# Row softmax on one core: one loop over a ring of twelve groups, a first load of 16 rows a partition, and late loads together behind two stores

## The chip, the core and the metric

The kernel runs on one core of a Trainium2 chip. The metric is device time in microseconds (us) of one execution of the program. The page and the trace of the profiled execution count from that execution's first instruction; their last instant is called the span.

The engines that matter: VectorE (DVE in the profile) does row maxima, reciprocals and most of the scaling; ScalarE (ACT) does the exponentials; GpSimd (POOL) does some of the scaling; SyncE (SP) issues every load and store; TensorE (PE) computes nothing and is used only for synchronization.

## The reference

The computation is a softmax along the last axis of a float32 array of 16 x 1024 rows with 512 elements each, 33.55 MB in and as much out.

```python
def reference(x):                                   # x: (16, 1024, 512) float32
    x_max = np.max(x, axis=-1, keepdims=True)
    exp_x = np.exp(x - x_max)
    return exp_x / np.sum(exp_x, axis=-1, keepdims=True)
```

## The kernel before

The 16,384 rows are cut into 16 groups. A group is 8 rows on each of the 128 partitions, 2 MB. Consecutive groups are bundled into chunks (`SIZES`), and a chunk is what one load and one store move: 2 MB or 4 MB. Everything stays in place: the load writes a group's rows into SBUF, the exponential and the scaling overwrite them, and the store reads them.

Four steps are done for each group.

- `rowmax` (line 145, VectorE): the negated maxima of 8 rows, or of 16 rows at once for the chunks that `WHOLE` names. It waits for the chunk's load.
- `exp` (line 134, ScalarE): eight activations, one for each row of a partition, with the negated maximum as bias and the row's sum as a second output. In the trace each is an ACTIVATE and an ACTIVATION_READ_ACCUMULATOR.
- the reciprocal of the sums (line 159, VectorE), which waits until ScalarE has finished the group (`summed`).
- the multiplication of the rows by the reciprocals (line 164), on GpSimd for the groups in `ON_POOL` and on VectorE for the others. It waits for the reciprocal (`inverted`).

Group 0 has a tensor of its own, `first`, and code of its own: its maxima are line 186, its eight exponentials are written out in front of the loop, and its reciprocal (line 211), its multiplication (line 213) and its store come at the very end. The other 15 groups go through `ring`, which holds 11 groups. ScalarE handles them in a loop (`exps`, line 150), in which one iteration is one group.

The order on VectorE is written out by hand: in step g it takes the maxima of group g (unless they were taken with those of the group before) and then scales group g - 2 (`BEHIND`). A multiplication that belongs to GpSimd is issued there at that same point.

All loads and stores go through SP's one queue, in an order written out by hand. The first load is moved in front of the starting barrier (`loads_at_the_head`). The next six loads fill the ring. Then comes `ORDER`: stores as their chunks become ready, and between them the two late loads (chunks 7 and 8), which go to places in the ring that an earlier store must have emptied (`BEFORE`). SP handles one thing after another, so whatever stands behind a wait of SP waits as well. A store waits for two counts, `by_vector` and `by_pool`, of the multiplications that are done.

At the end SP waits for all the stores (`others`, line 219).

Of the kernel before, what the change touches and what calls it, by code (L numbers as in the profile page):

```python
# [7 lines left out]
F32 = mybir.dt.float32  # L8
EXP = mybir.ActivationFunctionType.Exp
AX = mybir.AxisListType.X  # L10
ACT, DVE, POOL, PE, SP = [
    getattr(mybir.EngineType, e) for e in ("Activation", "DVE", "Pool", "PE", "SP")
]


GROUP = 8


SIZES = [1, 2, 2, 2, 2, 2, 1, 2, 2]
CHUNKS = len(SIZES)  # L20
RING = 11
STARTS = [sum(SIZES[:k]) for k in range(CHUNKS)]
GROUPS = sum(SIZES)

BEFORE = {7: 1, 8: 2}

ORDER = [
    ("store", 1),
    ("store", 2),
    ("load", 7),  # L30
    ("store", 3),
    ("load", 8),
    ("store", 4),
    ("store", 5),
    ("store", 6),
# [4 lines left out]
ON_POOL = [2, 4, 6, 8, 10, 12]  # L40

BEHIND = 2

WHOLE = (3, 4, 5)


AT_HEAD = {mybir.EngineType.SP: 1}
# [22 lines left out]
@with_exitstack  # L70
def kernel(
    ctx: ExitStack,
    tc: tile.TileContext,
    x: bass.AP,
    out: bass.AP,
):
    nc = tc.nc
    nc.at_finalize(loads_at_the_head)
    P = nc.NUM_PARTITIONS

    x_rows, out_rows = x.flatten_outer_dims(), out.flatten_outer_dims()
    d = x_rows.shape[1]
    assert x_rows.shape[0] == P * GROUPS * GROUP

    first = ctx.enter_context(nc.sbuf_tensor("first", [P, GROUP * d], F32))
    ring = ctx.enter_context(nc.sbuf_tensor("ring", [P, RING * GROUP * d], F32))

    def columns(name, n):
        return ctx.enter_context(nc.sbuf_tensor(name, [P, n], F32))


    first_stat, first_recip = columns("first_stat", GROUP), columns("first_recip", GROUP)
    stat, recip = columns("stat", RING * GROUP), columns("recip", RING * GROUP)

    def sem(name):
        return ctx.enter_context(nc.semaphore(name))

    maxima, summed, inverted, by_vector, by_pool = [
        sem(s) for s in ("maxima", "summed", "inverted", "by_vector", "by_pool")
    ]  # L100
    loaded = {k: sem(f"loaded{k}") for k in range(CHUNKS)}

    stored = {k: sem(f"stored{k}") for k in BEFORE.values()}
    others = sem("others")

    def at(g):
        return (g - 1) % RING

    def rows(g, groups=1):
        if g == 0:  # L110
            part = first[:, :]
        else:
            part = ring[:, at(g) * GROUP * d : (at(g) + groups) * GROUP * d]
        return part.rearrange("p (r d) -> p r d", d=d)

    def cols(t, g, groups=1):
        return t[:, at(g) * GROUP : (at(g) + groups) * GROUP]

    def in_dram(t, k):
        part = t[P * GROUP * STARTS[k] : P * GROUP * (STARTS[k] + SIZES[k]), :]  # L120
        return part.rearrange("(p r) d -> p r d", p=P)

    def load(k):
        return nc.sync.dma_start(  # L124
            out=rows(STARTS[k], SIZES[k]), in_=in_dram(x_rows, k)
        )

    def store(k):
        return nc.sync.dma_start(
            out=in_dram(out_rows, k), in_=rows(STARTS[k], SIZES[k])  # L130
        )

    def exp(row, one):
        return nc.scalar.activation(  # L134
            out=row, in_=row, func=EXP, bias=one, scale=1.0, accum_out=one
        )

    def spread(t):
        return t.unsqueeze(2).to_broadcast([P, GROUP, d])


    def rowmax(g, groups):
        k = max(c for c in range(CHUNKS) if STARTS[c] <= g)
        nc.vector.wait_ge(loaded[k], 16)
        nc.vector.reduce_max(  # L145
            out=cols(stat, g, groups), in_=rows(g, groups), axis=AX, negate=True
        ).then_inc(maxima, groups)

    def exps():
        with nc.Fori(0, GROUPS - 1, 1, engines=(ACT,)) as g:  # L150
            nc.scalar.wait_ge(maxima, 1).then_inc(maxima, -1)  # L151
            row = nc.scalar.snap((g % RING) * GROUP)
            for r in range(GROUP):
                done = exp(ring[:, bass.ds((row + r) * d, d)], stat[:, bass.ds(row + r, 1)])
            done.then_inc(summed, 1)

    def scale(g):
        nc.vector.wait_ge(summed, g)
        nc.vector.reciprocal(out=cols(recip, g), in_=cols(stat, g)).then_inc(inverted, 1)  # L159
        engine, scaled = nc.vector, by_vector  # L160
        if g in ON_POOL:
            engine, scaled = nc.gpsimd, by_pool
        engine.wait_ge(inverted, g)
        engine.tensor_mul(  # L164
            out=rows(g), in0=rows(g), in1=spread(cols(recip, g))
        ).then_inc(scaled, 1)

    def store_scaled(k):
        groups = STARTS[k] + SIZES[k] - 1
        on_pool = sum(g <= groups for g in ON_POOL)  # L170
        nc.sync.wait_ge(by_vector, groups - on_pool)
        if on_pool:
            nc.sync.wait_ge(by_pool, on_pool)  # L173
        store(k).then_inc(stored.get(k, others), 16)

    with tc.manual_schedule(engines={ACT, DVE, POOL, SP}):
        head = load(0)
        head.then_inc(loaded[0], 16)
        tc.info.no_tile_sem_insts.add(head.ins.name)
        nc.scalar.preload_act_table(EXP)  # L180
        with tc.tile_critical(sync_engine=SP):  # L181
            for k in range(1, min(BEFORE)):
                load(k).then_inc(loaded[k], 16)
        nc.vector.wait_ge(loaded[0], 16)
        behind = [
            nc.vector.reduce_max(  # L186
                out=first_stat[:], in_=rows(0), axis=AX, negate=True
            )
        ]
        for r in range(GROUP):  # L190
            behind.append(exp(rows(0)[:, r, :], first_stat[:, r : r + 1]))
        with tc.tile_critical(sync_engine=PE):  # L192
            exps()
            seen = 1
            for g in range(1, GROUPS):
                if g == seen:
                    k = max(c for c in range(CHUNKS) if STARTS[c] <= g)
                    take = SIZES[k] if k in WHOLE else 1
                    rowmax(g, take)
                    seen += take  # L200
                if g > BEHIND:
                    scale(g - BEHIND)
            for g in range(GROUPS - BEHIND, GROUPS):
                scale(g)
            for what, k in ORDER:
                if what == "store":
                    store_scaled(k)
                else:
                    nc.sync.wait_ge(stored[BEFORE[k]], 16)
                    load(k).then_inc(loaded[k], 16)  # L210
        nc.vector.reciprocal(out=first_recip[:], in_=first_stat[:])  # L211
        behind.append(
            nc.vector.tensor_mul(out=rows(0), in0=rows(0), in1=spread(first_recip[:]))  # L213
        )
        behind.append(store(0))
        for one in behind:
            tc.declare_no_dep(one.ins, head.ins, reason="VectorE waits for loaded[0]")
        with tc.tile_critical(sync_engine=SP):
            nc.sync.wait_ge(others, 16 * (CHUNKS - 1 - len(stored)))


# [28 lines left out]
```

## Time and profile before

| | |
|---|---|
| median of 3 runs | 161.96 us (161.93 to 162.73) |
| the profiled execution: time / span | 162.86 us / 161.1 us |
| VectorE busy | 122.9 us (76%), 39 instructions |
| ScalarE busy | 92.5 us (57%), 257 instructions |
| GpSimd busy | 42.3 us (26%), 10 instructions |
| the DMA queue | 67.11 MB, 97.5% of 16 engines' span, mean 417 GB/s |

A row of the slices has 40 digits; each is the busy share of one slice of the span, in tenths, and a slice is about 4 us long. A row of a timeline gives start, duration, engine, source line, operation, what is written and read with its shape, and in brackets the idle time of the engine before it and what ended it. A row of the waits gives who waited for whom, then the total in us, how often, and the longest. "SPq" is SP's queue of DMA issues. Durations of overlapping instructions of one engine can overlap by about 0.1 us.

### The profile page before, as it was taken

To read this page: it belongs to the slowest core of one execution; us is meant where nothing else is said; L and a number is where in the kernel's file an instruction comes from. 1 tells how busy PE (TensorE), PEld (TensorE's weight loads), DVE (VectorE), ACT (ScalarE), POOL (GpSimd) and SP (SyncE) were. 2 spreads that over 40 slices of the span, in tenths; PEclk is the share of its full clock that TensorE was granted. 3 is DMA by queue.
4 is the path that set the end of the run, shared out by engine and by line. 5 is a ranking of instruction groups with operands and counts; after the bars stand their busy time and mean duration, and the time that the engine had idled before them with its cause. 6 is when DMAs were issued, how large, how long until landed. Compare 5 with 4: busy or idle time off the path is not lost.

```text
span 161.1 us, 611 instructions
## 1 busy us (share of the span) xinstructions
DVE 122.9 (76%) x39; ACT 92.5 (57%) x257; POOL 42.3 (26%) x10
## 2 busy tenths in 40 slices
DVE  0190599999999999999999999963999999900000
ACT  3009439998957995995999919970199600000000
POOL 0000000000970690393096019500295000000000
DMA  7999999999999999999999999999999999999990
GB/s 232 435 505 391 407 505 391 407 496 399 407 488 407 399 378 500 407 399 496 407 399 488 415 391 472 439 391 464 439 399 456 399 435 468 448 399 448 395 439 28
DMA packets 2592, 67.11 MB, mean 417 GB/s; under 512 B 288, under 2 KB 288, under 8 KB 288
## 3 DMA queue, kind: packets, MB, share of 16 engines
q1 hardware_dynamic: 2592, 67.11, 97.5%
HBM read 33.55 MB, written 33.55 MB: 417 GB/s over the span
## 4 chain that ended last, share of the span: by engine, by line
DMA 47%; DVE 30%; issue 5%; POOL 4%; SPq 0%; DVEq 0%
DMA ring<-in_x_dram 35%; DVE stat L145 14%; DMA out_dram<-ring 13%; DVE ring L164 13%; POOL ring L164 4%; DVE first L213 3%; DVE recip L159 1%; SPq L124 0%; DVE first_recip L211 0%; DVEq L192 0%; SPq L245 0%; DVEq L211 0%; SPq L173 0%; SPq L181 0%
## 5 line engine op out<-in xcount | busy, mean ns | idle before, releaser
L134 ACT ACTIVATE ring<-ring,stat x120 | 84.8, 709 | 24.2 <-ACTq L151 24.2
L145 DVE TENSOR_REDUCE stat<-ring 128x8 f32<-128x4096 f32 (+1 forms) x12 | 65.4, 5457 | 10.2 <-ACT first L134 6.0
L164 POOL TENSOR_TENSOR ring<-ring,recip 128x4096 f32<-128x4096 f32 x6 | 42.1, 7016 | 80.4 <-DVE recip L159 80.4
L164 DVE TENSOR_TENSOR ring<-ring,recip 128x4096 f32<-128x4096 f32 x9 | 47.4, 5266 | 0.3
L134 ACT ACTIVATION_READ_ACCUMULATOR ring<-ring,stat x120 | 22.6, 188 | 0.0
L134 ACT ACTIVATE first<-first,first_stat 128x512 f32<-128x512 f32 x8 | 5.7, 708 | 10.0 <-DVE first_stat L186 10.0
L186 DVE TENSOR_REDUCE first_stat<-first 128x8 f32<-128x4096 f32 x1 | 4.4, 4420 | 7.6 <-DMA first<-in_x_dram 7.6
L213 DVE TENSOR_TENSOR first<-first,first_recip 128x4096 f32<-128x4096 f32 x1 | 4.4, 4424 | 0.0
L159 DVE RECIPROCAL recip<-stat 128x8 f32<-128x8 f32 x15 | 2.9, 192 | 0.0
L180 ACT ACT_TABLE_LOAD x1 | 1.3, 1283 | 0.8 <-PEq L234 0.8
L134 ACT ACTIVATION_READ_ACCUMULATOR first<-first,first_stat 128x1 f32 x8 | 1.5, 187 | 0.0
L211 DVE RECIPROCAL first_recip<-first_stat 128x8 f32<-128x8 f32 x1 | 0.2, 203 | 0.2 <-issue 0.2
L234 POOL MEMSET const-float32-0.0<- 128x1 f32 x1 | 0.1, 98 | 0.2 <-issue 0.2
L234 POOL MEMSET const-bfloat16-1.0<- 128x1 bf16 x1 | 0.1, 102 | 0.0
L234 POOL MEMSET const-uint8-127<- 128x1 uint8 x1 | 0.1, 102 | 0.0
L234 POOL MEMSET const-float32-1.0<- 128x1 f32 x1 | 0.1, 98 | 0.0
## 6 DMA issues: line engine op xcount, KB each, us to landing
ring<-in_x_dram SPq DMA_DIRECT2D x7, 4096.0 KB, 30.1
out_dram<-ring SPq DMA_DIRECT2D x7, 4096.0 KB, 23.7
first<-in_x_dram SPq DMA_DIRECT2D x1, 2048.0 KB, 7.6
ring<-in_x_dram SPq DMA_DIRECT2D x1, 2048.0 KB, 57.9
out_dram<-ring SPq DMA_DIRECT2D x1, 2048.0 KB, 28.1
out_dram<-first SPq DMA_DIRECT2D x1, 2048.0 KB, 18.4
```

Of the source, the lines that this page charges most:

```text
L134: return nc.scalar.activation(out=row, in_=row, func=EXP, bias=one, scale=1.0, accum_out=one)
L145: nc.vector.reduce_max(out=cols(stat, g, groups), in_=rows(g, groups), axis=AX, negate=True).then_inc(maxima, groups)
L159: nc.vector.reciprocal(out=cols(recip, g), in_=cols(stat, g)).then_inc(inverted, 1)
L164: engine.tensor_mul(out=rows(g), in0=rows(g), in1=spread(cols(recip, g))).then_inc(scaled, 1)
L180: nc.scalar.preload_act_table(EXP)
L186: nc.vector.reduce_max(out=first_stat[:], in_=rows(0), axis=AX, negate=True)
L211: nc.vector.reciprocal(out=first_recip[:], in_=first_stat[:])
L213: nc.vector.tensor_mul(out=rows(0), in0=rows(0), in1=spread(first_recip[:]))
L234: nc = _bacc.Bacc("TRN2", target_bir_lowering=False, num_devices=1)
```

## The change

Group 0 loses its separate tensor and code. The ring holds 12 groups, all 16 groups go through ScalarE's loop, and group 0 takes the same path as the others, so its store is now the first one. The chunks are cut anew: the first load brings two groups (16 rows a partition), and chunks 0 to 4 begin on even groups. Before, chunks 1 to 5 began on odd groups. The chunks whose maxima are taken at once are now 3 and 4, groups 6 and 7, and 8 and 9; before they were groups 5 and 6, 7 and 8, and 9 and 10. The groups on GpSimd and the lag of two groups stay.

In SP's order, stores 0 and 1 come first, and then the three late loads (chunks 7, 8 and 9: four groups) in a row: load 7 waits for store 0, and loads 8 and 9 for store 1. The other stores follow. A store waits for one semaphore of its own chunk, which VectorE and GpSimd both count up.

The last store is issued behind the hand-written part. PE then waits for all stores but that one, two of them covered by the late loads' waits; the last one is waited for by the framework. The seven early loads are no longer a block with a synchronization of its own.

The order of VectorE's and GpSimd's instructions in the middle of the two programs reads as follows ("max(5,6)" is one maximum over the 16 rows of both groups).

```
before:  max(5,6)  recip 3  VectorE mul 3   recip 4 -> GpSimd mul 4   max(7,8)  recip 5  VectorE mul 5   recip 6 -> GpSimd mul 6
after:   max(6,7)  recip 4 -> GpSimd mul 4  recip 5  VectorE mul 5    max(8,9)  recip 6 -> GpSimd mul 6  recip 7  VectorE mul 7
```

```diff
@@ -15,21 +15,23 @@
 
 GROUP = 8
 
-
-SIZES = [1, 2, 2, 2, 2, 2, 1, 2, 2]
+SIZES = [2, 2, 2, 2, 2, 1, 1, 2, 1, 1]
+RING = 12
 CHUNKS = len(SIZES)
-RING = 11
 STARTS = [sum(SIZES[:k]) for k in range(CHUNKS)]
 GROUPS = sum(SIZES)
 
-BEFORE = {7: 1, 8: 2}
+BEFORE = {7: 0, 8: 1, 9: 1}
+
 
 ORDER = [
+    ("store", 0),
     ("store", 1),
+    ("load", 7),
+    ("load", 8),
+    ("load", 9),
     ("store", 2),
-    ("load", 7),
     ("store", 3),
-    ("load", 8),
     ("store", 4),
     ("store", 5),
     ("store", 6),
@@ -41,7 +43,7 @@
 
 BEHIND = 2
 
-WHOLE = (3, 4, 5)
+WHOLE = (3, 4)
 
 
 AT_HEAD = {mybir.EngineType.SP: 1}
@@ -82,35 +84,32 @@
     d = x_rows.shape[1]
     assert x_rows.shape[0] == P * GROUPS * GROUP
 
-    first = ctx.enter_context(nc.sbuf_tensor("first", [P, GROUP * d], F32))
-    ring = ctx.enter_context(nc.sbuf_tensor("ring", [P, RING * GROUP * d], F32))
-
-    def columns(name, n):
+    def sbuf(name, n):
         return ctx.enter_context(nc.sbuf_tensor(name, [P, n], F32))
 
-
-    first_stat, first_recip = columns("first_stat", GROUP), columns("first_recip", GROUP)
-    stat, recip = columns("stat", RING * GROUP), columns("recip", RING * GROUP)
+    ring = sbuf("ring", RING * GROUP * d)
+
+    stat = sbuf("stat", RING * GROUP)
+    recip = sbuf("recip", RING * GROUP)
 
     def sem(name):
         return ctx.enter_context(nc.semaphore(name))
 
-    maxima, summed, inverted, by_vector, by_pool = [
-        sem(s) for s in ("maxima", "summed", "inverted", "by_vector", "by_pool")
-    ]
+    maxima, summed, inverted = [sem(s) for s in ("maxima", "summed", "inverted")]
+    scaled = {k: sem(f"scaled{k}") for k in range(CHUNKS)}
     loaded = {k: sem(f"loaded{k}") for k in range(CHUNKS)}
 
-    stored = {k: sem(f"stored{k}") for k in BEFORE.values()}
+    stored = {k: sem(f"stored{k}") for k in set(BEFORE.values())}
     others = sem("others")
 
+    def chunk_of(g):
+        return max(k for k in range(CHUNKS) if STARTS[k] <= g)
+
     def at(g):
-        return (g - 1) % RING
+        return g % RING
 
     def rows(g, groups=1):
-        if g == 0:
-            part = first[:, :]
-        else:
-            part = ring[:, at(g) * GROUP * d : (at(g) + groups) * GROUP * d]
+        part = ring[:, at(g) * GROUP * d : (at(g) + groups) * GROUP * d]
         return part.rearrange("p (r d) -> p r d", d=d)
 
     def cols(t, g, groups=1):
@@ -140,14 +139,13 @@
 
 
     def rowmax(g, groups):
-        k = max(c for c in range(CHUNKS) if STARTS[c] <= g)
-        nc.vector.wait_ge(loaded[k], 16)
+        nc.vector.wait_ge(loaded[chunk_of(g)], 16)
         nc.vector.reduce_max(
             out=cols(stat, g, groups), in_=rows(g, groups), axis=AX, negate=True
         ).then_inc(maxima, groups)
 
     def exps():
-        with nc.Fori(0, GROUPS - 1, 1, engines=(ACT,)) as g:
+        with nc.Fori(0, GROUPS, 1, engines=(ACT,)) as g:
             nc.scalar.wait_ge(maxima, 1).then_inc(maxima, -1)
             row = nc.scalar.snap((g % RING) * GROUP)
             for r in range(GROUP):
@@ -155,50 +153,36 @@
             done.then_inc(summed, 1)
 
     def scale(g):
-        nc.vector.wait_ge(summed, g)
+        nc.vector.wait_ge(summed, g + 1)
         nc.vector.reciprocal(out=cols(recip, g), in_=cols(stat, g)).then_inc(inverted, 1)
-        engine, scaled = nc.vector, by_vector
-        if g in ON_POOL:
-            engine, scaled = nc.gpsimd, by_pool
-        engine.wait_ge(inverted, g)
+        engine = nc.gpsimd if g in ON_POOL else nc.vector
+        engine.wait_ge(inverted, g + 1)
         engine.tensor_mul(
             out=rows(g), in0=rows(g), in1=spread(cols(recip, g))
-        ).then_inc(scaled, 1)
+        ).then_inc(scaled[chunk_of(g)], 1)
 
     def store_scaled(k):
-        groups = STARTS[k] + SIZES[k] - 1
-        on_pool = sum(g <= groups for g in ON_POOL)
-        nc.sync.wait_ge(by_vector, groups - on_pool)
-        if on_pool:
-            nc.sync.wait_ge(by_pool, on_pool)
+        nc.sync.wait_ge(scaled[k], SIZES[k])
         store(k).then_inc(stored.get(k, others), 16)
 
     with tc.manual_schedule(engines={ACT, DVE, POOL, SP}):
-        head = load(0)
-        head.then_inc(loaded[0], 16)
-        tc.info.no_tile_sem_insts.add(head.ins.name)
         nc.scalar.preload_act_table(EXP)
-        with tc.tile_critical(sync_engine=SP):
-            for k in range(1, min(BEFORE)):
-                load(k).then_inc(loaded[k], 16)
-        nc.vector.wait_ge(loaded[0], 16)
-        behind = [
-            nc.vector.reduce_max(
-                out=first_stat[:], in_=rows(0), axis=AX, negate=True
-            )
-        ]
-        for r in range(GROUP):
-            behind.append(exp(rows(0)[:, r, :], first_stat[:, r : r + 1]))
+
+
+        for k in range(min(BEFORE)):
+            first = load(k).then_inc(loaded[k], 16)
+            tc.info.no_tile_sem_insts.add(first.ins.name)
+            tc.add_to_no_dep_group("loads", first.ins)
+        tc.declare_fence(nc.sync.nop().ins, group="loads")
         with tc.tile_critical(sync_engine=PE):
             exps()
-            seen = 1
-            for g in range(1, GROUPS):
+            seen = 0
+            for g in range(GROUPS):
                 if g == seen:
-                    k = max(c for c in range(CHUNKS) if STARTS[c] <= g)
-                    take = SIZES[k] if k in WHOLE else 1
+                    take = SIZES[chunk_of(g)] if chunk_of(g) in WHOLE else 1
                     rowmax(g, take)
                     seen += take
-                if g > BEHIND:
+                if g >= BEHIND:
                     scale(g - BEHIND)
             for g in range(GROUPS - BEHIND, GROUPS):
                 scale(g)
@@ -208,15 +192,10 @@
                 else:
                     nc.sync.wait_ge(stored[BEFORE[k]], 16)
                     load(k).then_inc(loaded[k], 16)
-        nc.vector.reciprocal(out=first_recip[:], in_=first_stat[:])
-        behind.append(
-            nc.vector.tensor_mul(out=rows(0), in0=rows(0), in1=spread(first_recip[:]))
-        )
-        behind.append(store(0))
-        for one in behind:
-            tc.declare_no_dep(one.ins, head.ins, reason="VectorE waits for loaded[0]")
-        with tc.tile_critical(sync_engine=SP):
-            nc.sync.wait_ge(others, 16 * (CHUNKS - 1 - len(stored)))
+            nc.sync.wait_ge(scaled[CHUNKS - 1], SIZES[CHUNKS - 1])
+        store(CHUNKS - 1)
+        with tc.tile_critical(sync_engine=PE):
+            nc.tensor.wait_ge(others, 16 * (CHUNKS - 1 - len(stored)))
 
 
 # ---- launch: one core; inputs and outputs as the reference has them ----
```

## The prediction

> **What bounds the kernel now.** I read the slices of the page first, then the queue line, then what the queue's engine waited for, then the timelines of VectorE and GpSimd.
>
> ```profile
> DVE  0190599999999999999999999963999999900000
> POOL 0000000000970690393096019500295000000000
> DMA  7999999999999999999999999999999999999990
> GB/s 232 435 505 391 407 505 391 407 496 399 407 488 407 399 378 500 407 399 496 407 399 488 415 391 472 439 391 464 439 399 456 399 435 468 448 399 448 395 439 28
> q1 hardware_dynamic: 2592, 67.11, 97.5%
> ```
>
> The DMA row has no slice under 9 between the first and the last: one queue moves 33.55 MB in and 33.55 MB out without a hole. VectorE, busy 122.9 us of 161.1, is the second; it has idle slices at both ends and a dip near 105 us. So the end is set by bytes as long as every store is ready before the queue runs dry; compute matters only by the deadlines it sets for stores.
>
> ```profile
> DVE stat L145 <- DMA ring<-in_x_dram: 4.2, 2, 4.0
> SPq L245 <- DMA out_dram<-first: 17.8, 1, 17.8
> ```
>
> The first line (waits) says VectorE stood 4.0 us for a late load, so it was ahead of the queue there. The second (the queue's own waits): SP had issued the last store 17.8 us before it landed. That is the slack at the end of the kernel before.
>
> The pace: the first load (2 MB) lands at 7.59, the third at 26.96 in the chain (five 2 MB units in), so one unit takes (26.96 - 7.59)/4 = 4.84 us. The last store lands at 159.7 (issued 141.25, 18.4 to landing), 1.4 us before the span's end.
>
> ```profile
> 66.68 0.20 DVE L159 RECIPROCAL recip<-stat 128x8 f32<-128x8 f32 x1
> 66.80 8.63 DVE L145 TENSOR_REDUCE stat<-ring 128x16 f32<-128x8192 f32 x1
> 75.35 0.19 DVE L159 RECIPROCAL recip<-stat 128x8 f32<-128x8 f32 x1
> 75.57 4.42 DVE L164 TENSOR_TENSOR ring<-ring,recip 128x4096 f32<-128x4096 f32 x1
> 79.92 0.20 DVE L159 RECIPROCAL recip<-stat 128x8 f32<-128x8 f32 x1
> 80.03 4.37 DVE L145 TENSOR_REDUCE stat<-ring 128x8 f32<-128x4096 f32 x1
> 84.31 0.19 DVE L159 RECIPROCAL recip<-stat 128x8 f32<-128x8 f32 x1
> 84.54 6.95 DVE L164 TENSOR_TENSOR ring<-ring,recip 128x4096 f32<-128x4096 f32 x1
> 91.41 4.41 DVE L145 TENSOR_REDUCE stat<-ring 128x8 f32<-128x4096 f32 x1
> ```
>
> ```profile
> 66.96 7.01 POOL L164 TENSOR_TENSOR ring<-ring,recip 128x4096 f32<-128x4096 f32 x1 [6.22 <-DVE recip L159]
> 80.19 7.02 POOL L164 TENSOR_TENSOR ring<-ring,recip 128x4096 f32<-128x4096 f32 x1 [6.22 <-DVE recip L159]
> ```
>
> This is the row that decides. A GpSimd multiply starts 0.27 us after the reciprocal that frees it (66.68 to 66.96) and takes 7.02. The double maximum at 66.80 runs its usual 8.63 beside it. But VectorE's multiply at 84.54 meets the GpSimd one of 80.19 and takes 6.95 in place of 4.42: it ends at 91.49, which is 4.28 after GpSimd's end (87.21). The same holds at 100.35 (GpSimd ends 103.02, VectorE 107.30) and at 120.22 (122.89, 127.17). So VectorE's multiply does not share: it stands until GpSimd is through. In the kernel before, groups 4, 6 and 8 pay none of this, since a double maximum covers each of these GpSimd multiplies.
>
> **The change, part by part.**
>
> *First load of 16 rows.* 4 MB instead of 2: VectorE's first maximum starts at 7.59 + 4.84 = 12.43. Against that, VectorE no longer stands 6.02 us (to 18.03) until the eight separate exponentials are done. The queue starts as before.
>
> *One loop on ScalarE.* Same 128 exponentials, 5.65 us a group (22.81 to 28.46), 0.3 to 0.4 us from maximum to first exponential. ScalarE has 92.5 us of work; below, each reciprocal is checked against it and it is never last. Cost nothing.
>
> *Stores count per chunk.* One semaphore wait on SP instead of two, behind a full queue: nothing.
>
> *The order of VectorE and GpSimd.* The six groups on GpSimd stay 2 to 12 in steps of two, but chunks now begin on even groups. So a double maximum (groups 6,7, then 8,9) is followed by the reciprocals of groups 4 and 5 back to back, GpSimd's multiply of group 4, and VectorE's multiply of group 5 with nothing between: they start almost together. From the reciprocal of group 4: GpSimd + 0.27. VectorE: the next instruction issues 0.11 behind a reciprocal (66.68 to 66.80), and the multiply 0.23 behind its own reciprocal's start (75.35 to 75.57), so + 0.34. GpSimd is first by 0.07 us. I take it that the first holds the other off whole, as in the three rows above.
>
> No row shows so near a tie. Bounded: VectorE loses at most 7.02 (a whole GpSimd multiply) less the 0.07, at least 0 (it goes first and GpSimd stands). I take the loss, by the rows in which the one that started earlier won. The Trainium skill ("SBUF — State Buffer", section "Who interferes with whom") says that of a VectorE operation with two SBUF inputs and a GpSimd one that reads SBUF, the one issued first keeps the shared port for its whole instruction. By that rule 0.07 us is enough, and it gives the same sum; only the other order of issue would give that of the first rival below, and no row here shows who wins a tie.
>
> VectorE's clock, then, with 4.33 from a single maximum to the next instruction (80.03 to 84.31 and alike), 8.55 from a double one, 4.34 from a multiply, 4.20 from GpSimd's end when it stood:
> - maxima of groups 0, 1: 12.43 to 21.09; load 1 lands at 12.43 + 9.68 = 22.1.
> - group 2's maximum and 0's multiply, 3's and 1's: 2 x (4.33 + 0.23 + 4.34) = 17.8, to 39.9.
> - groups 4,5 singly: 4.33 + 0.27 + 7.02 + 4.20 = 15.82 a pair (VectorE's multiply stands for GpSimd's, as at 84.54), to 55.75.
> - groups 6,7 and 8,9, double maxima: 8.55 + 0.27 + 7.02 + 4.20 = 20.04 each, to 95.8. In the kernel before, such a pair takes 13.24 (53.56 to 66.80).
> - groups 10,11; 12,13; 14,15 singly: 3 x 15.82 = 47.5, to 143.3. There group 13's multiply ends.
>
> Waits of SP: store 7 (groups 12, 13) is issued at 143.4. The queue reaches the end of what is ahead of it, 28 of 32 units, at 159.7 - 4 x 4.84 = 140.3. It is dry. The stores before it make it: store 1 (56 against 61), 2 (76 against 101), 3 (96 against 111), 4 (112 against 121), 6 (128 against 135). Store 8 and 9 (148, 152.6 and under 1 us of hand-over) come while store 7 runs.
>
> From issue to an empty queue: the first load needs 7.59 for 4.84 us of data, 2.75 over. The other bound is SP's issue alone, 0.33 (the store's row in SP's timeline). I take 2.75, the one row of a queue that starts empty. Last landing: 143.4 + 2.75 + 4 x 4.84 = 165.5. The Trainium skill ("DMA: Bandwidth & Descriptors", section "Anatomy of one DMA") gives a fixed cost of about 2.0 us for a DMA on another issue path; by it the sum would be an estimated 0.75 us lower.
>
> *Late loads together.* SP waits for store 0 (about 71.4, where the first wait of this kind ended before), issues load 7, then waits for store 1 (about 81.1) with loads 8, 9 and all later stores queued behind it. Load 7's two units keep the queue full to about 91, so nothing is lost; without that cover it is one restart, 2.75. VectorE needs them at 111.6 and later; they land near 91 to 101. The queue turns between reading and writing three times instead of five. The windows 12 to 40, 90 to 111 and 111 to 141 us give 433, 424 and 436 GB/s: the mixed stretch is about 2% slower over 21 us, 0.4 us. Gain between 0 and 0.4; I take 0.2 where the queue stays full, none where it runs dry.
>
> *The end.* PE instead of SP waits for the other stores, and the separate step for group 0 (reciprocal 0.2, multiply 4.42, store) is gone from the end. Of the 1.4 us behind the last landing some waits of SP go, others on PE come: between -0.7 (half of it) and +0.3; I take -0.2.
>
> Span: 165.5 + 1.38 - 0.2 = 166.7, against 161.1. That profiled execution took 162.86, 1.8 over its span, and the median is 161.96, 0.89 over that span; I carry the median's difference: 166.7 + 0.9 = 167.6.
>
> **Rivals.**
> *VectorE goes first at the ties (not slower).* Place: the multiplies of groups 5 and 7. For it: 0.07 us is small, and a start in the trace need not be the moment the operand is read; against: the three rows. A double pair then takes 8.55 + 0.34 + 4.34 = 13.23; 82.2 after both, GpSimd runs late to 96.3 for group 8, VectorE's next multiply waits for that to 100.5, then two pairs of 15.82: store 7 is issued at 132.2, 8 us ahead of 140.3. Queue full, time 161.96 - 0.2 - 0.2 = 161.6. It decides as soon as store 7 is issued before about 140.3 - 2.75 = 137.5.
> *One tie each way.* 6.8 us back: store 7 at 136.6, just in time: 161.6, at most 1 more.
> *The queue runs dry elsewhere.* If load 7's cover failed at 81 while VectorE won its ties, one restart: 161.6 + 2.75 = 164.3. The DMA row speaks against it: SP waited twice for stores before (16.9 us in all) without a hole.
> *The end does not get shorter.* If SP still walks its waits behind PE's, the 0.2 is lost or turns to +0.3; it moves every case and changes none.
>
> **How the numbers follow.** Forecast 0.66, VectorE first 0.25, one each 0.06, dry elsewhere 0.03. The forecast's own range: 165.0 (restart at 0.33 and the better end, 164.9) to 168.5 (0.9 more if the profiled execution's distance from its span holds). The whole range reaches down to 161.0 to take in most of the second case; under it lie 0.08, over it 0.08. What a measurement of this kernel can tell from no change is about 0.5%, 0.8 us. Faster (under 161.15): 0.10 of the second case and 0.01 of the third, 0.11. Within: 0.14 + 0.04 = 0.18. Slower: 0.66 + 0.01 + 0.01 + 0.03 = 0.71.
>
> **What would show it.** Right: VectorE multiplies of about 11.3 us at about 64.6 and 84.7, a hole in the DMA row of 4 to 5 us near 142 to 146, SP's wait for store 7 as the last long one, and VectorE's first maximum at 12.4. Wrong: GpSimd multiplies of 11 us there instead, multiplies of VectorE at 4.4, and a DMA row of nines to the end.

## The result, and the profile after

The changed kernel takes 167.56 us (median of 4, 167.41 to 167.64) against 162.25 us of the kernel before in the same comparison: 1.032 times as long (95% interval 1.029 to 1.036), 5.3 us slower. Its profiled execution took 167.53 us with a span of 165.7 us.

The slices and the queue line of the changed kernel:

```profile
DVE  0009979999999999999999999999999999998000
POOL 0000000000294004920059107900970195000000
DMA  7989999899999999999989999999999993299894
GB/s 269 482 388 467 419 411 475 380 482 403 443 443 388 431 415 411 427 459 395 483 388 423 423 451 459 395 483 403 443 427 407 423 439 138 127 435 451 380 443 190
q1 hardware_dynamic: 2880, 67.11, 95.0%
```

Its waits (who waited for whom: total us, times, longest), VectorE's for the loads, then the largest of SP's queue:

```profile
DVE stat L143 <- DMA ring<-in_x_dram: 13.3, 2, 12.3
```

```profile
SPq L128 <- DVE ring L160: 104.1, 7, 36.0
```

The DMA row now has a hole: 3 and 2 in the 34th and 35th slice, 138 and 127 GB/s, which is 137 to 145 us. VectorE shows the opposite: once started at 12.3 us it has no idle slice, and after its first maxima it no longer waits for a load, except 1.0 us for the second one (13.3 in all, 12.3 of it the first). SP's queue waits longest for VectorE's multiplies. Such a wait costs something only where it leaves the queue dry.

VectorE's and GpSimd's timelines in the stretch of the double maxima:

```profile
55.65 8.67 DVE L143 TENSOR_REDUCE stat<-ring 128x16 f32<-128x8192 f32 x1
64.25 0.25 DVE L157 RECIPROCAL recip<-stat 128x8 f32<-128x8 f32 x2
64.54 11.28 DVE L160 TENSOR_TENSOR ring<-ring,recip 128x4096 f32<-128x4096 f32 x1
75.73 8.67 DVE L143 TENSOR_REDUCE stat<-ring 128x16 f32<-128x8192 f32 x1
84.33 0.26 DVE L157 RECIPROCAL recip<-stat 128x8 f32<-128x8 f32 x2
84.62 11.28 DVE L160 TENSOR_TENSOR ring<-ring,recip 128x4096 f32<-128x4096 f32 x1
95.82 4.41 DVE L143 TENSOR_REDUCE stat<-ring 128x8 f32<-128x4096 f32 x1
```

```profile
64.52 7.02 POOL L160 TENSOR_TENSOR ring<-ring,recip 128x4096 f32<-128x4096 f32 x1 [13.06 <-DVE recip L157]
84.60 7.02 POOL L160 TENSOR_TENSOR ring<-ring,recip 128x4096 f32<-128x4096 f32 x1 [13.06 <-DVE recip L157]
```

A tie is the case in which both engines' multiplies are released at almost the same moment. Both ties went to GpSimd, by 0.02 us. Its multiplies keep their 7.02 us; VectorE's take 11.28 instead of 4.42 and end 4.28 us behind GpSimd's (64.52 + 7.02 + 4.28 = 75.82 = 64.54 + 11.28). This is what became of the two 8.6 us maxima that covered GpSimd in the kernel before.

SP's timeline around store 7, with its issue and those of the last two stores merged in one row:

```profile
143.37 9.82 SPq L128 DMA_DIRECT2D out_dram<-ring  x3
```

Store 7 is issued at 143.37. By the trace's packets the queue had moved its last byte at 139.0; the first packet of store 7 starts at 144.2. The hole is 5.2 us, nearly all that the kernel lost.

### The profile page after: what moved, and what is told of

It is laid out like the page before. It is cut to its first block, busy times and chain, and to the rows that moved or that the text cites. A ratio compares the mean times of both kernels' runs of the same rounds, so it can differ in the third digit from the quotient of the medians.

```text
span 165.7 us, 609 instructions
## 1 busy us (share of the span) xinstructions
DVE 138.9 (84%) x40; ACT 92.5 (56%) x257; POOL 42.3 (26%) x10
## 4 chain that ended last, share of the span: by engine, by line
DVE 68%; DMA 13%; issue 11%
DVE stat L143 37%; DVE ring L160 30%; DMA ring<-in_x_dram 13%; DVE recip L157 1%
## 5 line engine op out<-in xcount | busy, mean ns | idle before, releaser
L133 ACT ACTIVATE ring<-ring,stat x128 | 90.4, 709 | 50.3 <-ACTq L149 50.3
L143 DVE TENSOR_REDUCE stat<-ring 128x8 f32<-128x4096 f32 (+1 forms) x14 | 70.0, 5006 | 13.3 <-DMA ring<-in_x_dram 13.3
L160 DVE TENSOR_TENSOR ring<-ring,recip 128x4096 f32<-128x4096 f32 x10 | 68.0, 6804 | 0.3
L133 ACT ACTIVATION_READ_ACCUMULATOR ring<-ring,stat x128 | 24.1, 188 | 0.0
```

Source lines behind the costliest of these rows:

```text
L133: return nc.scalar.activation(out=row, in_=row, func=EXP, bias=one, scale=1.0, accum_out=one)
L143: nc.vector.reduce_max(out=cols(stat, g, groups), in_=rows(g, groups), axis=AX, negate=True).then_inc(maxima, groups)
L160: engine.tensor_mul(out=rows(g), in0=rows(g), in1=spread(cols(recip, g))).then_inc(scaled[chunk_of(g)], 1)
```

## The experiments

All edits are to the changed kernel unless said otherwise. The kernel before differed more between its own executions (161.8 to 164.4 us over all of them) than any variant with its late loads in a row, so the variants are compared by their own times. "Store 7" is the store of groups 12 and 13. For the queue to stay full it must be issued by about 138.1, an estimate: store 6 landed at 139.5, and a dry queue took 1.4 us to restart (shown below).

**1. Take the ties away: single maxima.**

```diff
-WHOLE = (3, 4)
+WHOLE = ()
```

> Edit: no maxima over two groups at once, so a single maximum stands between GpSimd's and VectorE's multiply everywhere. Theory (two tied multiplies make store 7 late): no multiply of VectorE over 7 us; each of the two pairs takes 15.8 us instead of 20.1, store 7 is issued at 143.4 - 2 x 4.3 = 134.8, before the 138.1 at which the queue would still take it without a hole (139.5, where store 6 lands, less the 1.4 of a restart). Last landing 139.5 + 19.4 = 158.9, time 162.2 (161.6 to 162.8). Rival (the late loads together, or the first load of 4 MB by itself, cost the time): 167 to 168, since both stay.

161.95 us (161.78 to 162.17), 0.996 of the kernel before (0.993 to 0.998). VectorE's and GpSimd's timelines and the DMA slices:

```profile
59.90 0.19 DVE L157 RECIPROCAL recip<-stat 128x8 f32<-128x8 f32 x1
60.01 4.36 DVE L143 TENSOR_REDUCE stat<-ring 128x8 f32<-128x4096 f32 x1
64.30 0.19 DVE L157 RECIPROCAL recip<-stat 128x8 f32<-128x8 f32 x1
64.52 6.95 DVE L160 TENSOR_TENSOR ring<-ring,recip 128x4096 f32<-128x4096 f32 x1
```

```profile
60.17 7.02 POOL L160 TENSOR_TENSOR ring<-ring,recip 128x4096 f32<-128x4096 f32 x1 [8.80 <-DVE recip L157]
```

```profile
DMA  7999999999998999999999999999999999999993
```

The same work in smaller maxima: about 4.2 us of GpSimd's 7.02 (60.17 to 67.19) lie beside a maximum, VectorE's multiply stands only for the rest (6.95 in all), VectorE's busy time falls from 138.9 to 130.3 us, and the hole is gone. All 5.6 us went with it, though the late loads, the first load of 4 MB and the one loop are all still there.

**2. Keep the double maxima, but let VectorE go first.**

```diff
+SWAPPED = (4, 6)
...
-    def scale(g):
+    def invert(g):
         nc.vector.wait_ge(summed, g + 1)
         nc.vector.reciprocal(out=cols(recip, g), in_=cols(stat, g)).then_inc(inverted, 1)
+
+    def multiply(g, count):
         engine = nc.gpsimd if g in ON_POOL else nc.vector
-        engine.wait_ge(inverted, g + 1)
+        engine.wait_ge(inverted, count)
...
+    def scale(g):
+        if g in SWAPPED:
+            invert(g + 1)
+            invert(g)
+            multiply(g + 1, g + 1)
+            multiply(g, g + 2)
+        elif g - 1 not in SWAPPED:
+            invert(g)
+            multiply(g, g + 1)
```

> Edit: for groups 4,5 and 6,7 the reciprocal of the odd group is taken first, so VectorE's multiply can start about 0.1 us behind the second reciprocal and GpSimd's about 0.27. Theory (whoever starts first keeps the other off for its whole multiply): VectorE's two multiplies take 4.4, GpSimd's two about 11.3; a double pair takes about 13.2; store 7 issued near 132 to 133, time 162.2 (161.6 to 162.8). Rival (VectorE always yields to GpSimd, whoever starts): multiplies of 11.3 on VectorE, 167.5.

162.03 us (161.81 to 162.21). VectorE's and GpSimd's timelines:

```profile
64.17 0.26 DVE L159 RECIPROCAL recip<-stat 128x8 f32<-128x8 f32 x2
64.39 4.42 DVE L164 TENSOR_TENSOR ring<-ring,recip 128x4096 f32<-128x4096 f32 x1
68.73 8.68 DVE L145 TENSOR_REDUCE stat<-ring 128x16 f32<-128x8192 f32 x1
77.33 0.26 DVE L159 RECIPROCAL recip<-stat 128x8 f32<-128x8 f32 x2
77.56 4.43 DVE L164 TENSOR_TENSOR ring<-ring,recip 128x4096 f32<-128x4096 f32 x1
...
90.85 9.26 DVE L164 TENSOR_TENSOR ring<-ring,recip 128x4096 f32<-128x4096 f32 x1
```

```profile
64.50 11.19 POOL L164 TENSOR_TENSOR ring<-ring,recip 128x4096 f32<-128x4096 f32 x1 [13.13 <-DVE recip L159]
77.67 11.19 POOL L164 TENSOR_TENSOR ring<-ring,recip 128x4096 f32<-128x4096 f32 x1 [1.98 <-DVE recip L159]
```

The order of two 0.2 us reciprocals turns the tie round: VectorE starts 0.11 us ahead and pays nothing, GpSimd takes 11.19 (7.02 + 4.17). So it is who starts first, not which engine. GpSimd does not pay for nothing: its multiply of group 8 then runs until 95.8, and VectorE's multiply at 90.85 stands for it, 9.26 us instead of 6.95. That is far less than two ties lost, and store 7 is issued at 131.8, well ahead of the deadline. It is the prediction's first rival, brought about by hand; the prediction's price for it was 161.6.

**3. One tie instead of two.**

```diff
-WHOLE = (3, 4)
+WHOLE = (3,)
```

> Edit: only groups 6 and 7 have their maxima taken at once; one tie is left. Theory: store 7 is issued at 143.4 - 4.3 = 139.1, lands 11.1 later at 150.2 instead of 149.2 without a hole: a hole of about 1 us, time 163.2 (162.6 to 163.8). Rival (each tie costs the end its full share): half way, 164.9. Rival (DMA order or first load): 167.5.

163.22 us (163.05 to 163.47). SP's timeline and the DMA slices:

```profile
138.88 9.81 SPq L128 DMA_DIRECT2D out_dram<-ring  x3
```

```profile
DMA  7999999999999999999999999999999999899994
```

Store 7 is issued 4.5 us earlier, 0.8 us past the deadline, and only an 8 is left in the row. One tie costs 1.3 us (163.22 - 161.95), the second 4.3 us (167.56 - 163.22). A cost beside a deadline isn't paid by the piece: the first part of it uses up the slack.

**4. The late loads spread as before, ties kept.**

```diff
     ("load", 7),
-    ("load", 8),
-    ("load", 9),
     ("store", 2),
+    ("load", 8),
     ("store", 3),
+    ("load", 9),
     ("store", 4),
```

> Edit: the three late loads are spread, one behind each of stores 1, 2 and 3, as the kernel before does it. Theory: both ties stay, store 7 is issued at 143.4 as before the edit, time 167.5 (167.0 to 168.0). Rival (three late loads in a row, with SP standing for store 1, starve the queue or the stores): 162 to 164.

167.45 us (167.34 to 167.51): no difference. SP standing for store 1 with all else queued behind it isn't what starves the queue.

**5. An early start, ties kept.**

```diff
-SIZES = [2, 2, 2, 2, 2, 1, 1, 2, 1, 1]
+SIZES = [1, 1, 1, 1, 2, 2, 2, 1, 1, 2, 1, 1]
...
-BEFORE = {7: 0, 8: 1, 9: 1}
+BEFORE = {9: (0, 1), 10: (2, 3), 11: (2, 3)}
...
-WHOLE = (3, 4)
+WHOLE = (5, 6)
...
-                    nc.sync.wait_ge(stored[BEFORE[k]], 16)
+                    for one in BEFORE[k]:
+                        nc.sync.wait_ge(stored[one], 16)
```

In `ORDER` stores 0 to 3 come first, then loads 9 to 11, then the other stores.

> Edit: groups 0 to 3 are loaded and stored one by one (2 MB each), the rest as in the changed kernel, both ties kept. Theory (VectorE's end is a chain of standing times, and the first load of 4 MB adds to it): VectorE takes group 2's maxima at about 17.3 instead of 22.0, everything behind it is 4.7 us earlier, store of groups 12, 13 issued at 138.7, landing 11.1 later at 149.8 (149.2 without a hole): time 162.9 (162.3 to 163.5), although VectorE's two multiplies still take 11.3. Rival (the ties alone are to blame and the late start is covered): 167.5.

163.16 us (162.94 to 163.21). VectorE's timeline at the start, then SP's for store 7:

```profile
7.89 4.42 DVE L134 TENSOR_REDUCE stat<-ring 128x8 f32<-128x4096 f32 x1 [7.89 <-DMA ring<-in_x_dram]
12.74 4.42 DVE L134 TENSOR_REDUCE stat<-ring 128x8 f32<-128x4096 f32 x1 [0.43 <-DMA ring<-in_x_dram]
17.64 4.42 DVE L134 TENSOR_REDUCE stat<-ring 128x8 f32<-128x4096 f32 x1 [0.48 <-DMA ring<-in_x_dram]
```

```profile
138.99 9.82 SPq L119 DMA_DIRECT2D out_dram<-ring  x3
```

Group 2's maximum starts at 17.64 instead of 22.03, and store 7 follows 4.4 us earlier, with both 11.27 us multiplies still in place. So the ties alone do not make the loss: the late start and the ties together carry store 7 past its deadline, and undoing either takes most of it away. What the late start delays is VectorE's third instruction, which waits for the second 4 MB load, not the first.

This start is not that of the kernel before, which took its first maximum at 7.59 but then stood until 18.03. Against that kernel the ties weigh most. Group 13's multiply ends at 143.3 instead of 127.2, 16.2 us later, and the two double pairs of 20.1 us instead of 13.2 make 13.7 of it. The other 2.5 us are the net of all the rest (the start, group 0's scaling no longer at the end, one double maximum less); no run separates them.

**6. The other groups on GpSimd, double maxima kept.**

```diff
-ON_POOL = [2, 4, 6, 8, 10, 12]
+ON_POOL = [3, 5, 7, 9, 11, 13]
```

> Edit: GpSimd takes groups 3, 5, ..., 13 instead of 2, 4, ..., 12, so each GpSimd multiply between the double maxima lies beside a maximum. Theory: no tie there, multiplies of 4.4 on VectorE for groups 4 and 6; one new tie at the very end (groups 13, 14); store of groups 12, 13 issued at about 134.4, queue full, time 161.9 (161.5 to 162.4). Rival (GpSimd's share as such or the double maxima cost): 164 or more.

162.02 us (161.88 to 162.35). VectorE's timeline:

```profile
61.98 4.42 DVE L160 TENSOR_TENSOR ring<-ring,recip 128x4096 f32<-128x4096 f32 x1
...
75.22 4.42 DVE L160 TENSOR_TENSOR ring<-ring,recip 128x4096 f32<-128x4096 f32 x1
...
127.30 11.27 DVE L160 TENSOR_TENSOR ring<-ring,recip 128x4096 f32<-128x4096 f32 x1
```

VectorE's multiplies of groups 4 and 6 take 4.42; the new tie of groups 13 and 14 is at 127.30, 11.27 us long, and costs nothing that the time shows (162.02 against 161.95 in experiment 1): store 7 is issued at 134.3, and the last two stores at 138.6 and 143.5 follow while the queue is still busy with it. So neither the double maxima nor GpSimd's share is at fault, only their phase.

**7. The same ties in the kernel before.**

```diff
-ON_POOL = [2, 4, 6, 8, 10, 12]
+ON_POOL = [1, 3, 5, 7, 9, 11]
```

> Edit to the kernel before: GpSimd takes groups 1, 3, ..., 11, so that three ties arise there. Theory: three VectorE multiplies of about 11.3, 6.8 us lost at each; store of groups 12, 13 issued at about 143.6, groups 14, 15 at about 152.7 and group 0 at about 157.5; last landing near 169.3, time 172.5 (171.5 to 173.5). Rival (the slack at the end of the kernel before, 17.8 us, absorbs it): 162 to 163.5.

172.73 us (172.68 to 172.92), 1.057 times the kernel before (1.052 to 1.062). VectorE's timeline, then the DMA slices:

```profile
52.04 11.27 DVE L164 TENSOR_TENSOR ring<-ring,recip 128x4096 f32<-128x4096 f32 x1
...
72.12 11.27 DVE L164 TENSOR_TENSOR ring<-ring,recip 128x4096 f32<-128x4096 f32 x1
...
92.20 11.27 DVE L164 TENSOR_TENSOR ring<-ring,recip 128x4096 f32<-128x4096 f32 x1
```

```profile
DMA  7999999999999999999999999998985802899995
```

Three ties, and a hole of the same kind, 136.8 to 144.9 by the trace's packets. Nothing of the change is in this kernel but the phase between GpSimd's groups and the double maxima.

**8. SP instead of PE waits at the end** (on top of single maxima).

```diff
-        with tc.tile_critical(sync_engine=PE):
-            nc.tensor.wait_ge(others, 16 * (CHUNKS - 1 - len(stored)))
+        with tc.tile_critical(sync_engine=SP):
+            nc.sync.wait_ge(others, 16 * (CHUNKS - 1 - len(stored)))
```

> Edit: as single_maxima (no maxima over two groups), and SP instead of PE waits at the end for all stores but the last. Theory (the place of this wait costs nothing either way): 1.4 us from the last landing to the end of the span, time 161.95 (161.7 to 162.2). Rival (PE's wait saves what the prediction took): 0.2 us or more longer behind the last landing.

161.77 us (161.65 to 161.98), 0.990 of the kernel before (0.987 to 0.993): the lowest median here, but its range overlaps that of experiment 1 (161.78 to 162.17), which ran on another chip, so the times alone do not show a gain. The traces do show a difference: from the last landing to the span's end there are 1.29 us with SP here, and 1.44 to 1.45 in all nine traces in which PE waits. So the wait on PE takes about 0.15 us longer. The expectation's time held, its tail of 1.4 us with no difference did not; the rival was wrong in sign.

**9 and 10. Loads in a row or spread, with a full queue.** The first kernel is that of experiment 1; the second adds the diff of experiment 4 to it.

> The same kernel as single_maxima (three late loads in a row, queue full), beside spread_single on one chip. Theory (each turn of the queue from loads to stores delays it): store 6 lands near 139.4, time 161.9 (161.7 to 162.2).

> Edit to single_maxima: late loads spread behind stores 1, 2 and 3. Theory (each turn from loads to stores costs some tenths): store 6 lands at about 140.2 as in spread_loads, 0.7 later than with loads in a row, and with a full queue this reaches the end: 162.6 (162.3 to 163.3), and a wider spread of times between runs. Rival (the order of loads does not matter with a full queue): 161.9, as loads_in_a_row within 0.2.

161.96 us (161.86 to 162.37) in a row, 162.56 (162.27 to 163.35) spread; against the kernel before 0.993 (0.990 to 0.996) and 0.998 (0.996 to 1.000). In the trace store 6 lands at 139.2 and 140.1. The late loads in a row are worth about 0.6 us and steadier times. In the changed kernel the gain is there too, but hidden: its queue's last packet before the hole ends at 139.0, that of experiment 4 at 139.7, and both then wait for the same store 7.

## Why the prediction was right

*The ties.* Predicted: GpSimd first by 0.07 us, two multiplies of about 11.3 us at 64.6 and 84.7. Measured: first by 0.02 us, 11.28 us at 64.54 and 84.62. Experiment 2 shows that the order of starting decides; the step that was only taken from rows further apart is now shown. One reading on the way was wrong: in the kernel before, the double maxima cover the GpSimd multiplies of groups 2, 4 and 6, not 4, 6 and 8. Group 8's is the one at 80.19 that makes VectorE's multiply at 84.54 take 6.95. Nothing in the sum rests on it, since the pair of 13.24 us is read from the right rows.

*VectorE's clock.* Every station of the sum came within 0.2 us: 39.9 (39.83), 55.75 (55.65), 95.8 (95.82), 143.3 (143.26), and store 7 at 143.4 (143.37).

*When the queue runs dry.* Predicted 140.3 for store 6's landing, measured 139.5; the hole lies at 139.0 to 144.2, where the prediction looked for it near 142 to 146. The term that was mis-sized is the gain of the loads in a row: taken at 0.2 us and as nothing where the queue runs dry; the runs give 0.6 to 0.9. In this kernel nothing came of it, as the prediction said. The 17.8 us that the prediction calls the slack at the end of the kernel before are more than the slack: the last store was issued at 141.25, and what stood ahead of it in the queue had landed by 154.8, so the queue would have run dry 13.6 us after that issue. The forecast does not use the figure.

*The restart.* Taken at 2.75 us, by the first load. Store 7 needed 11.1 us to land, 9.7 of them data: 1.4 us. The first load isn't a fair row for this. In the kernel before, its first packets of 16 KB took 0.9 to 1.8 us against 0.61 later on (in the changed kernel most of the first of 32 KB took 1.6 to 2.3 against 1.21), while store 7's took 1.21 to 1.25 from the first. The 2.75 put the last landing at 165.5; it was 164.3.

*The end.* Taken at -0.2 us, measured +0.06 against the kernel before (1.44 and 1.38 us), and by experiment 8 the wait on PE is even slower than the same on SP.

*From span to time.* I added 0.9 us, the distance of the median from the span of one profiled execution. The part outside the span is 1.8 us in every profiled execution (167.53 and 165.7 here; 162.86 and 161.1 before); the kernel before merely had a slower execution profiled than its median. So two errors of sizing stood against each other: the span came out 1.0 us too long (166.7 to 165.7) and the part outside it 0.95 too short. That the sum of 167.6 meets 167.56 so closely is luck; with 1.8 us it would have been 168.5. At the low end of the range the better terms add up to 164.7, not to the 164.9 written there; nothing else rests on it.

*The rivals.* VectorE first gives 162.0 when it is arranged (experiment 2). One tie each way did not occur and was not made; experiment 3 is not the same case, since single maxima (15.8 us a pair) stand there in place of the tie that VectorE would win (13.2). The queue had no other hole. What the prediction said of the first load was right in size and stands in its sum, but it does not name it as a part of the cause: experiment 5 shows that undoing it alone takes away 4.4 of the 5.6 us between experiment 1 and the changed kernel.

## What to carry to other kernels

Where two engines exclude each other, look at what lies beside each of the slower engine's operations, not at busy shares: here both kernels do nearly the same work, and a shift of the groups by one put two multiplies side by side that a reduction had kept apart. Then ask which deadline the loss meets; walk the last stores back from the end at the queue's pace, and the issue time of the first one that is late gives the whole time. Work out the part outside the span from the profiled execution's own time, not from the median.

## What the runs showed of the hardware

- 0.02 us of lead decides over 7 us: 64.52 against 64.54, and VectorE stands for all of GpSimd's multiply. It went the same way in all eleven ties of these traces in which GpSimd led by 0.02 to 0.03 us; with 0.11 us of lead the other way, GpSimd's takes 11.19 us.
- The queue that had run dry took 1.4 us to restart (first packet 0.8 us after the issue), half of what the first load of the program costs over its data (2.75).
- The late loads put one by one between stores cost about 0.6 us more than the same loads in a row, with times that varied more: 162.27 to 163.35 against 161.86 to 162.37.
- The same wait at the end of the program takes about 0.15 us longer on PE (1.44 us from the last landing to the span's end) than on SP (1.29).
